# Strided attention on one core: four heads as one contiguous block, keys and values prepared once, one DMA queue in a fixed order

## The chip, the cores and the metric

The kernel runs on one core of a Trainium2 chip. The core has a matmul engine (TensorE, PE in the profile, its weight loads PEld), a vector engine (VectorE, DVE), an engine for activations and copies (ScalarE, ACT), GpSimd (POOL), and SyncE (SP), which here only issues transfers; sixteen DMA engines move data between the device memory and the on-chip memory (SBUF). Matmuls write to a second on-chip memory, PSUM, which has eight banks. The metric is the time of one execution in microseconds (us); lower is better. Before the change it is 152.51 us, the median of three runs (152.01 to 153.02).

## The reference

Each of the 1024 queries of each of the 8 × 12 heads attends to 16 keys, those at every 64th position. All arrays are float32.

```python
batch, heads, seq, dim = (8, 12, 1024, 64)      # stride 64
scale = 1.0 / np.sqrt(dim)
for i in range(seq):
    attend_positions = np.arange(0, seq, stride)
    q = Q[:, :, i:i + 1, :].copy()
    k = K[:, :, attend_positions, :].copy()
    v = V[:, :, attend_positions, :].copy()
    scores = np.einsum('bhqd,bhkd->bhqk', q, k) * scale
    weights = np.exp(scores - np.max(scores, axis=-1, keepdims=True))
    weights = weights / (np.sum(weights, axis=-1, keepdims=True) + 1e-10)
    result[:, :, i, :] = np.einsum('bhqk,bhkd->bhqd', weights, v)[:, :, 0, :]
```

Q and the result are 25.17 MB each; the rows of K and V that are used are 0.39 MB each. Arithmetic is small, so nearly all the data that moves is Q in and the result out.

## The kernel before

The work is cut into 24 groups of four heads (loops over `b` and `g0`). For each group one DMA loads 1 MiB of Q (`qn`, line 111): partition p of 128 holds, for each of the four heads, query rows 8p to 8p+7, so a partition receives four rows of 2 KiB, one from each head. Two small DMAs (lines 116 and 121) load the group's 64 key rows and 64 value rows of 256 bytes. All loads are issued by SP, the store of the result by ACT (line 221).

The values are used as bf16 by reading the upper half of each float32 in place. Per group, in the order in which the program names them:

- Four matmuls (lines 127 and 135) with 0/1 matrices `r_top` and `r_bot` spread the keys (transposed) and the values into a block layout in PSUM, `kv_psum`; ScalarE copies it to SBUF as `kv_sb` (line 144). A pair of query rows sits in one 128-partition column block, so the block layout holds every head's keys twice, for the upper and the lower 64 rows.
- Sixteen 128 × 128 transposes on TensorE (line 154) turn Q into `qt_psum`, which takes two PSUM banks and has one buffer. One ScalarE copy of 2048 columns (line 160) moves it to `qt_all`.
- Four score matmuls (line 166), one for each head, each in its own 32-column strip of the array and 512 columns long. ScalarE takes the exponential with the scale (line 175) into `w1t`. The maximum is not subtracted.
- Four matmuls with a 0/1 selector `s_sel` (line 179) give the sums, and VectorE takes their reciprocals (line 188).
- For each of the four heads, four output matmuls (line 193) with 32 rows of weights and 128 columns, into one PSUM bank of two, and two VectorE multiplies of 256 elements by the reciprocals (line 210), into `out_sb`.

Q has four buffers, `qt_all`, the kv tiles, `w1t` and `out_sb` three each. The order in which each engine runs its instructions is not the order of the program: a planner reorders the work of neighbouring groups, so transposes of one group stand among the output matmuls of another. Waits between engines are set from the tiles that are read and written. A DMA waits at its issuing engine: on SP a load whose buffer is not free holds back what is issued behind it.

Of the kernel before, what the change touches and what calls it, by code (L numbers as in the profile page):

```python
# [11 lines left out]
FP32 = mybir.dt.float32  # L13
BF16 = mybir.dt.bfloat16
# [10 lines left out]

@with_exitstack
def kernel(
# [8 lines left out]
    nc = tc.nc  # L36
# [6 lines left out]
    G = 4  # L43
    RPP = S // P
    NT = RPP // 2
    CH = S // (2 * P)
    assert H % G == 0 and RPP == 8 and NK == 16

    const_pool = ctx.enter_context(tc.tile_pool(name="const", bufs=1))
    qn_pool = ctx.enter_context(tc.tile_pool(name="qn", bufs=4))  # L50
    qt_pool = ctx.enter_context(tc.tile_pool(name="qt", bufs=3))
    kv_pool = ctx.enter_context(tc.tile_pool(name="kv", bufs=3))
    w_pool = ctx.enter_context(tc.tile_pool(name="w", bufs=3))
    out_pool = ctx.enter_context(tc.tile_pool(name="outsb", bufs=3))
    rec_pool = ctx.enter_context(tc.tile_pool(name="rec", bufs=2 * G))
    psum_sc = ctx.enter_context(tc.tile_pool(name="psc", bufs=2, space=bass.MemoryType.PSUM))
    psum_o = ctx.enter_context(tc.tile_pool(name="po", bufs=2, space=bass.MemoryType.PSUM))
    psum_sums = ctx.enter_context(tc.tile_pool(name="psums", bufs=1, space=bass.MemoryType.PSUM))
    psum_qt = ctx.enter_context(tc.tile_pool(name="pqt", bufs=1, space=bass.MemoryType.PSUM))
    psum_kv = ctx.enter_context(tc.tile_pool(name="pkv", bufs=1, space=bass.MemoryType.PSUM))  # L60

    identity = const_pool.tile([P, P], BF16, name="identity")
    make_identity(nc, identity)

    col_idx = const_pool.tile([P, P], I16, name="col_idx")
    nc.gpsimd.iota(col_idx, pattern=[[1, P]], base=0, channel_multiplier=0)
    iota_p = const_pool.tile([P, 1], I16, name="iota_p")
    nc.gpsimd.iota(iota_p, pattern=[[0, 1]], base=0, channel_multiplier=1)  # L68

    p_shr4 = const_pool.tile([P, 1], I16, name="p_shr4")  # L70
    nc.vector.tensor_scalar(  # L71
        out=p_shr4, in0=iota_p, scalar1=4, scalar2=None, op0=ALU.logical_shift_right
    )
    p_shr4_f32 = const_pool.tile([P, 1], FP32, name="p_shr4_f32")
    nc.vector.tensor_copy(out=p_shr4_f32, in_=p_shr4)
    target_i16 = const_pool.tile([P, 1], I16, name="target_i16")
    nc.vector.tensor_scalar(
        out=target_i16, in0=p_shr4, scalar1=16.0, scalar2=None, op0=ALU.mult
    )
    nc.vector.tensor_tensor(out=target_i16, in0=target_i16, in1=iota_p, op=ALU.add)  # L80
    target_f32 = const_pool.tile([P, 1], FP32, name="target_f32")
    nc.vector.tensor_copy(out=target_f32, in_=target_i16)
    target_bot_f32 = const_pool.tile([P, 1], FP32, name="target_bot_f32")
    nc.vector.tensor_scalar(
        out=target_bot_f32, in0=target_f32, scalar1=16.0, scalar2=None, op0=ALU.add
    )

    r_top = const_pool.tile([P, P], BF16, name="r_top")
    nc.vector.tensor_scalar(
        out=r_top, in0=col_idx, scalar1=target_f32, scalar2=None, op0=ALU.is_equal  # L90
    )
    r_bot = const_pool.tile([P, P], BF16, name="r_bot")
    nc.vector.tensor_scalar(
        out=r_bot, in0=col_idx, scalar1=target_bot_f32, scalar2=None, op0=ALU.is_equal
    )

    col_idx8 = const_pool.tile([P, 2 * G], I16, name="col_idx8")
    nc.gpsimd.iota(col_idx8, pattern=[[1, 2 * G]], base=0, channel_multiplier=0)
    s_sel = const_pool.tile([P, 2 * G], BF16, name="s_sel")
    nc.vector.tensor_scalar(  # L100
        out=s_sel, in0=col_idx8, scalar1=p_shr4_f32, scalar2=None, op0=ALU.is_equal
    )

    for b in range(B):
        for g0 in range(0, H, G):
            qn = qn_pool.tile([P, G, RPP, D], FP32, name="qn", tag="qn")
            q_src = _ap_with(
                Q[b, g0],
                [[RPP * D, P], [S * D, G], [1, RPP * D]],
            )  # L110
            nc.sync.dma_start(qn, q_src)
            qn_bf = qn.bitcast(BF16)
            qn_pitch = G * RPP * 2 * D

            k_raw = kv_pool.tile([G * NK, D], FP32, name="k_raw", tag="k_raw")
            nc.sync.dma_start(k_raw, K[b, g0 : g0 + G, ::stride, :])
            k_bf = k_raw.bitcast(BF16)
            k_hi = _ap_with(k_bf, [k_bf.ap[0], [2, D]], extra_offset=1)

            v_raw = kv_pool.tile([G * NK, D], FP32, name="v_raw", tag="v_raw")  # L120
            nc.sync.dma_start(v_raw, V[b, g0 : g0 + G, ::stride, :])
            v_bf = v_raw.bitcast(BF16)
            v_hi = _ap_with(v_bf, [v_bf.ap[0], [2, D]], extra_offset=1)

            kv_psum = psum_kv.tile([P, 2 * P], FP32, name="kv_psum", tag="kv_psum")
            for hp, rmat in enumerate((r_top, r_bot)):
                nc.tensor.matmul(  # L127
                    kv_psum[64 * hp : 64 * hp + D, 0:P],
                    lhsT=k_hi,
                    rhs=rmat[0 : G * NK, :],  # L130
                    start=True,
# [125 lines left out]
```

## Time and profile before

The profiled execution has a span of 150.7 us from the first to the last instruction. No separate time of that execution is given beside its span; the median of the runs is 152.51 us, 1.8 us above it.

| | |
|---|---|
| median of 3 runs | 152.51 us (152.01 to 153.02) |
| profiled execution, span | 150.7 us |
| TensorE matmul busy | 126.9 us (84%), 1056 instructions |
| VectorE busy | 79.9 us (53%) |
| ScalarE busy | 67.0 us (44%) |
| GpSimd busy | 1.1 us (1%) |
| moved by DMA | 51.29 MB, mean 340 GB/s over the span |

How to read it. The page has the busy time of each engine, the span cut into 40 slices (busy tenths of each engine, and GB/s), the DMA queues, the chain of work that ended last, and the costliest groups of instructions. A group's row reads: line, engine, operation, output<-input by name, shapes, count, then total busy us and the mean ns of one, then the idle time of the engine just before these instructions and what ended most of it. The chain is followed back from the last instruction, at each step to what released it; in order of time, each piece has its start, its length, and the engine and line. A window's row has, for a stretch of the span, the busy us of each engine with its count of instructions, the granted TensorE clock, the share of the sixteen DMA engines that was busy, and GB/s. A timeline's row has a start, a length, the engine and line, what is written and read, and how many instructions are merged. Matmuls overlap in the array, so the busy time of TensorE is more than the time that the array needs, and idle time of an engine that is not the bottleneck costs nothing.

### The profile page before, as it was taken

How to read it: one execution, taken by the hardware profiler on the slowest of the kernel's cores; microseconds unless marked ns; L12 is line 12 of the kernel's file. 1: busy time of each engine (PE TensorE's matmuls, PEld its weight loads, DVE VectorE, ACT ScalarE, POOL GpSimd, SP SyncE). 2: the span in 40 equal slices, each digit the busy share in tenths (PEclk: the TensorE clock that was granted, in tenths of full speed). 3: DMA queues.
4: the chain of work that ended last, by engine and by line, in shares of the span. 5: the costliest groups of instructions: out<-in, count | busy, mean ns of one | idle time of the engine just before them, and what ended most of it. 6: DMA issues, size and time to landing. Idle time of an engine off the chain costs nothing.

```text
span 150.7 us, 2715 instructions
## 1 busy us (share of the span) xinstructions
PE 126.9 (84%) x1056; PEld 84.2 (56%) x1056; DVE 79.9 (53%) x225; ACT 67.0 (44%) x73; POOL 1.1 (1%) x9
## 2 busy tenths in 40 slices
PE   0279889989989989989989989989989989987630
PEld 0246656646646647647647647647647647646210
DVE  3004575565565565565565565564564564574650
ACT  3063547147147147147147147147147147147100
POOL 2000000000000000000000000000000000000000
DMA  4999999999999999999999999999999987257266
GB/s 133 347 358 367 363 391 407 280 316 398 397 405 404 408 397 404 406 398 379 397 388 376 385 364 378 384 388 357 387 372 358 389 313 295 102 182 278 99 232 226
DMA packets 29196, 51.29 MB, mean 340 GB/s; under 512 B 4608, under 2 KB 4608, under 8 KB 29184
## 3 DMA queue, kind: packets, MB, share of 16 engines
q1 hardware_dynamic: 16512, 25.96, 49.3%
q10 hardware_dynamic: 12672, 25.17, 43.5%
q8 instruction: 8, 0.13, 0.3%
q14 instruction: 4, 0.03, 0.1%
HBM read 25.95 MB, written 25.17 MB: 339 GB/s over the span
## 4 chain that ended last, share of the span: by engine, by line
PE 73%; ACT 17%; DMA 4%; DVE 2%; issue 1%; DVEq 0%; ACTq 0%
PE qt_psum L154 31%; PE out L193 21%; ACT qt_all L160 16%; PE scores L166 13%; DMA qn<-in_Q_dram 4%; PE kv_psum L127 4%; PE kv_psum L135 3%; DVE out_sb L210 2%; PE sums_psum L179 2%; ACT w1t L175 0%; DVEq L252 0%; ACTq L160 0%; ACTq L175 0%
## 5 line engine op out<-in xcount | busy, mean ns | idle before, releaser
L210 DVE TENSOR_TENSOR out_sb<-out,recip 128x256 f32<-128x256 f32 x192 | 70.0, 418 | 20.6 <-PE out L193 20.2
L160 ACT COPY qt_all<-qt_psum 128x2048 bf16<-128x2048 bf16 x24 | 44.8, 1866 | 34.9 <-PE qt_psum L154 30.8
L154 PE MATMUL qt_psum<-identity,qn 128*128 128x128 bf16 x384 | 49.4, 311 | 6.4 <-DMA qn<-in_Q_dram 6.4
L154 PEld LDWEIGHTS <-qn 128*128 128x128 bf16 x384 | 37.8, 141 | 20.8 <-DMA qn<-in_Q_dram 11.2
L193 PE MATMUL out<-kv_sb,w1t 32*128 32x128 bf16 x384 | 42.7, 302 | 2.0 <-DVE out_sb L210 1.7
L188 DVE RECIPROCAL recip<-sums_psum 128x32 f32<-128x32 f32 x24 | 8.6, 358 | 43.2 <-PE sums_psum L179 43.2
L193 PEld LDWEIGHTS <-w1t 32*128 32x128 bf16 x384 | 24.2, 125 | 12.0 <-DVE out_sb L210 8.9
L175 ACT ACTIVATE w1t<-scores 128x512 bf16<-128x512 f32 x24 | 14.3, 597 | 32.7 <-PE scores L166 17.9
L166 PE MATMUL scores<-qt_all,kv_sb 128*32 128x512 bf16 x96 | 21.5, 604 | 7.8 <-ACT qt_all L160 7.8
L166 PEld LDWEIGHTS <-kv_sb 128*32 128x32 bf16 x96 | 5.0, 101 | 14.2 <-issue 13.9
L144 ACT CAST kv_sb<-kv_psum 128x256 bf16<-128x256 f32 x24 | 8.9, 372 | 6.4 <-PE kv_psum L135 6.4
L127 PEld LDWEIGHTS <-k_raw 64*64 64x64 bf16 x48 | 5.9, 124 | 6.3 <-issue 2.6
L127 PE MATMUL kv_psum<-r_top,k_raw 64*64 64x128 bf16 x24 | 7.5, 312 | 0.8 <-DMA k_raw<-in_K_dram 0.8
L179 PEld LDWEIGHTS <-w1t 128*128 128x128 bf16 x96 | 7.3, 127 | 1.3 <-ACT w1t L175 1.3
L179 PE MATMUL sums_psum<-s_sel,w1t 128*128 128x8 bf16 x96 | 7.0, 179 | 0.8 <-ACT w1t L175 0.8
L127 PE MATMUL kv_psum<-r_bot,k_raw 64*64 64x128 bf16 x24 | 7.4, 310 | 0.0
L135 PE MATMUL kv_psum<-v_raw,r_bot 64*128 64x64 bf16 x24 | 5.6, 233 | 0.0
L135 PE MATMUL kv_psum<-v_raw,r_top 64*128 64x64 bf16 x24 | 5.5, 231 | 0.0
L135 PEld LDWEIGHTS <-r_bot 64*128 64x128 bf16 x24 | 2.5, 103 | 2.8
L135 PEld LDWEIGHTS <-r_top 64*128 64x128 bf16 x24 | 2.5, 102 | 2.8
L144 ACT ACT_TABLE_LOAD x1 | 1.3, 1283 | 0.7 <-PEq L238 0.7
L71 DVE TENSOR_SCALAR p_shr<-iota_p 128x1 int16<-128x1 int16 x1 | 0.2, 156 | 1.6 <-POOL iota_p L68 1.6
(17 smaller groups left out, 2.9 us busy)
## 6 DMA issues: line engine op xcount, KB each, us to landing
qn<-in_Q_dram SPq DMA_DIRECT2D x24, 1024.0 KB, 8.6
out_dram<-out_sb ACTq DMA_DIRECT2D x24, 1024.0 KB, 8.3
k_raw<-in_K_dram SPq DMA_DIRECT2D x24, 16.0 KB, 7.8
v_raw<-in_V_dram SPq DMA_DIRECT2D x24, 16.0 KB, 7.4
```

Of the source, the lines that this page charges most:

```text
L71: nc.vector.tensor_scalar(out=p_shr4, in0=iota_p, scalar1=4, scalar2=None, op0=ALU.logical_shift_right)
L127: nc.tensor.matmul(kv_psum[64 * hp : 64 * hp + D, 0:P], lhsT=k_hi, rhs=rmat[0 : G * NK, :], start=True, stop=True, tile_position=(0, 64 * hp),
L135: nc.tensor.matmul(kv_psum[:, P + 64 * hp : P + 64 * hp + D], lhsT=rmat[0 : G * NK, :], rhs=v_hi, start=True, stop=True, tile_position=(0, 0),
L144: nc.scalar.copy(kv_sb, kv_psum)
L154: nc.tensor.transpose(qt_psum[:, (gi * NT + t) * P : (gi * NT + t + 1) * P], lhsT, identity,)
L160: nc.scalar.copy(qt_all, qt_psum)
L166: nc.tensor.matmul(scores[32 * gi : 32 * gi + 32, :], lhsT=kv_sb[:, 32 * gi : 32 * gi + 32], rhs=qt_all[:, 512 * gi : 512 * (gi + 1)], sta ...
L175: nc.scalar.activation(out=w1t, in_=scores, func=AF.Exp, bias=0.0, scale=scale)
L179: nc.tensor.matmul(sums_psum[:, c, :], lhsT=w1t[:, c * P : (c + 1) * P], rhs=s_sel, start=True, stop=True, tile_position=(0, 0),)
L188: nc.vector.reciprocal(recip, sums_psum)
L193: nc.tensor.matmul(out1[:, c, :, :], lhsT=w1t[32 * gi : 32 * gi + 32, c * P : (c + 1) * P], rhs=kv_sb[32 * gi : 32 * gi + 32, P : 2 * P], ...
L210: nc.vector.tensor_tensor(out=dst, in0=out1[:, :, e, :], in1=recip_b, op=ALU.mult,)
```

## The change

The kernel is written anew around the same arithmetic.

- **Blocks.** Four heads of 1024 queries are 4096 consecutive query rows, 1 MiB in one piece. Partition p now holds 32 consecutive query rows, one run of 8 KiB. The head of a row therefore depends on the partition (32 partitions for a head) and no longer on the place within it.
- **Loads and stores.** Q has eleven buffers and the result nine. All DMAs are issued by SP: keys, values, eleven loads, then for each group its store and the load of the group eleven ahead. The result leaves in an order in which a partition has two runs of 4 KiB.
- **Keys and values once.** The used rows of all 96 heads come in two DMAs of 1536 rows of 256 bytes, ahead of Q. GpSimd makes permutations from the identity, and bf16 copies. Twelve matmuls and six ScalarE copies put the keys into `k_t`; four matmuls and sixteen VectorE multiplies by a 0/1 `mask` put the values into `v_bd`, for each group a 128 × 256 matrix that has each head's values in the rows of that head alone.
- **Weights.** The exponentials are written into one of three buffers, zeroed once, by two activations of 64 partitions each, so that the two halves stand on the diagonal of each 128 × 128 block and zeros stand elsewhere. Score matmuls read Q in runs of 32 columns. Sums take eight matmuls of 4 columns instead of four of 8; outputs eight of 128 rows and 256 columns instead of sixteen of 32 rows and 128 columns; VectorE's multiplies are four of 512 elements instead of eight of 256.
- **Order.** `tc.manual_schedule()` leaves the order as written. For group g: sums, outputs 0 and 1, scores of g+1, output 2, the first half of the transposes of g+2, output 3, the second half. The transposed Q goes through PSUM in halves of 1024 columns with two buffers; output banks are three.

```diff
...
+    HG = 4
+    NG = B * H // HG
+    NC = NG // 2
+    SD = S * D
+    assert B * H == NG * HG and S == 1024 and D == 64 and NK == 16
+    QBUFS = 11
+    OBUFS = 9
+    const = ctx.enter_context(tc.tile_pool(name="const", bufs=1))
+    qn_pool = ctx.enter_context(tc.tile_pool(name="qn", bufs=QBUFS))
+    out_pool = ctx.enter_context(tc.tile_pool(name="outsb", bufs=OBUFS))
+    qt_pool = ctx.enter_context(tc.tile_pool(name="qt", bufs=2))
+    rec_pool = ctx.enter_context(tc.tile_pool(name="rec", bufs=2))
+    psum_qt = ctx.enter_context(tc.tile_pool(name="pqt", bufs=2, space=bass.MemoryType.PSUM))
     psum_sc = ctx.enter_context(tc.tile_pool(name="psc", bufs=2, space=bass.MemoryType.PSUM))
...
+    psum_o = ctx.enter_context(tc.tile_pool(name="po", bufs=3, space=bass.MemoryType.PSUM))
+    psum_s = ctx.enter_context(tc.tile_pool(name="psm", bufs=1, space=bass.MemoryType.PSUM))
+    ctx.enter_context(tc.manual_schedule())
+    k_raw = const.tile([P, NC, D], FP32, name="k_raw")
+    v_raw = const.tile([P, NC, D], FP32, name="v_raw")
+    kv_src = [[stride * D, P], [2 * HG * SD, NC], [1, D]]
+    nc.sync.dma_start(k_raw, _ap_with(K, kv_src))
+    nc.sync.dma_start(v_raw, _ap_with(V, kv_src))
+    qn = {}
+    def load(g):
+        qn[g] = qn_pool.tile([P, 32 * D], FP32, name="qn", tag="qn")
+        nc.sync.dma_start(qn[g], _ap_with(Q, [[32 * D, P], [1, 32 * D]], g * HG * SD))
+    for g in range(QBUFS):
+        load(g)
+    identity = const.tile([P, P], BF16, name="identity")
     make_identity(nc, identity)
...
+    id_v = identity.rearrange("p (c b a k) -> p c b a k", c=2, b=2, a=2)
+    perm_k = const.tile([P, 2, 2, 2, NK], BF16, name="perm_k")
+    perm_v = const.tile([P, 2, 2, 2, 2, NK], BF16, name="perm_v")
+    for c in range(2):
+        for a in range(2):
+            nc.gpsimd.tensor_copy(out=perm_k[:, c, a], in_=id_v[:, c, :, a])
+    k_dup = const.tile([P, NC, 2, D], BF16, name="k_dup")
+    for e in range(2):
+        nc.gpsimd.tensor_copy(out=k_dup[:, :, e], in_=k_raw)
+    for c in range(2):
+        for a in range(2):
+            for e in range(2):
+                nc.gpsimd.tensor_copy(
+                    out=perm_v[:, c, a, :, e], in_=id_v[:, c, :, a]
+                )
+    v_bf = const.tile([P, NC, D], BF16, name="v_bf")
+    nc.gpsimd.tensor_copy(out=v_bf, in_=v_raw)
+    k_t = const.tile([P, NC, 2, 4, 2, NK], BF16, name="k_t")
+    nc.vector.memset(k_t, 0.0)
+    w_bufs = []
+    for i in range(3):
+        w = const.tile([P, 8, P], BF16, name=f"w{i}")
+        nc.vector.memset(w, 0.0)
+        w_bufs.append(w)
+    iota_p = const.tile([P, 1], I16, name="iota_p")
     nc.gpsimd.iota(iota_p, pattern=[[0, 1]], base=0, channel_multiplier=1)
...
+    slot_i = const.tile([P, 1], I16, name="slot_i")
     nc.vector.tensor_scalar(
...
+        out=slot_i, in0=iota_p, scalar1=4, scalar2=3,
+        op0=ALU.logical_shift_right, op1=ALU.bitwise_and,
+    )
+    slot_f = const.tile([P, 1], FP32, name="slot_f")
+    nc.vector.tensor_copy(out=slot_f, in_=slot_i)
+    col4 = const.tile([P, 4], I16, name="col4")
+    nc.gpsimd.iota(col4, pattern=[[1, 4]], base=0, channel_multiplier=0)
+    s_sel = const.tile([P, 4], BF16, name="s_sel")
     nc.vector.tensor_scalar(
...
+        out=s_sel, in0=col4, scalar1=slot_f, scalar2=None, op0=ALU.is_equal
+    )
+    mask = const.tile([P, 4], FP32, name="mask")
     nc.vector.tensor_scalar(
...
+        out=mask, in0=col4, scalar1=slot_f, scalar2=None, op0=ALU.is_equal
+    )
+    pk = perm_k.rearrange("p c a b k -> p (c a b k)")
+    for n in range(NC // 4):
+        kp = psum_o.tile([P, 4, 2, 4, NK], FP32, name="kp", tag="o")
+        for i in range(4):
+            nc.tensor.matmul(
+                kp[:, i], lhsT=k_dup[:, 4 * n + i].rearrange("p e d -> p (e d)"),
+                rhs=pk, start=True, stop=True,
+            )
+        for e in range(2):
+            h = slice(64 * e, 64 * e + 64)
+            nc.scalar.copy(
+                k_t[h, 4 * n : 4 * n + 4, :, :, e].rearrange("p n c s k -> p (n c s) k"),
+                kp[h].rearrange("p n c s k -> p (n c s) k"),
+            )
+    v_bd = const.tile([P, NC, 2, 4, D], BF16, name="v_bd")
+    for n in range(2):
+        for c in range(2):
+            vp = psum_sc.tile([P, NC // 2, D], FP32, name="vp", tag="sc")
+            nc.tensor.matmul(
+                vp, lhsT=perm_v[:, c].rearrange("p a b e k -> p (a b e k)"),
+                rhs=v_bf[:, 6 * n : 6 * n + 6], start=True, stop=True,
+            )
+            for s in range(4):
+                nc.vector.tensor_scalar(
+                    out=v_bd[:, 6 * n : 6 * n + 6, c, s], in0=vp,
+                    scalar1=mask[:, s : s + 1], scalar2=None, op0=ALU.mult,
                 )
...
+    qt, wt, rec, out_sb = {}, {}, {}, {}
+    def transposes(g, x):
+        if x == 0:
+            qt[g] = qt_pool.tile([P, 2, 8, P], BF16, name="qt", tag="qt")
+        ps = psum_qt.tile([P, 8, P], BF16, name="qt_ps", tag="qt_ps")
+        qb = qn[g].bitcast(BF16)
+        for i in range(8):
+            nc.tensor.transpose(
+                ps[:, i],
+                _ap_with(qb, [qb.ap[0], [2, P]], extra_offset=(8 * x + i) * 2 * P + 1),
+                identity,
+            )
+        nc.scalar.copy(qt[g][:, x], ps)
+    def scores(g):
+        sc = psum_sc.tile([P, 512], FP32, name="sc", tag="sc")
+        q = qt[g]
+        kt = k_t[:, g // 2, g % 2].rearrange("p s e k -> p (s e k)")
+        for j in range(4):
+            a, b = divmod(j, 2)
+            nc.tensor.matmul(
+                sc[32 * j : 32 * j + 32],
+                lhsT=kt[:, 32 * j : 32 * j + 32],
+                rhs=_ap_with(
+                    q, [q.ap[0], [P, 8], [8 * P, 2], [1, 32]],
+                    extra_offset=32 * (2 * b + a),
+                ),
+                start=True, stop=True, tile_position=(0, 32 * j),
+            )
+        w = wt[g] = w_bufs[g % 3]
+        for a in range(2):
+            wa = w[64 * a : 64 * a + 64]
+            nc.scalar.activation(
+                out=_ap_with(wa, [wa.ap[0], [P, 8], [1, 2], [2, 32]], extra_offset=64 * a),
+                in_=sc[64 * a : 64 * a + 64].rearrange("p (t x q) -> p t x q", t=8, x=2),
+                func=AF.Exp, bias=0.0, scale=scale,
+            )
+    def sums(g):
+        sm = psum_s.tile([P, 2, 8, 2], FP32, name="sm", tag="sm")
+        for i in range(8):
+            nc.tensor.matmul(
+                sm[:, :, i], lhsT=wt[g][:, i], rhs=s_sel, start=True, stop=True
+            )
+        rec[g] = rec_pool.tile([P, 2, 16], FP32, name="rec", tag="rec")
+        nc.vector.reciprocal(rec[g], sm.rearrange("p b i e -> p b (i e)"))
+    def outputs(g, c):
+        if c == 0:
+            out_sb[g] = out_pool.tile([P, 2, 16, D], FP32, name="out_sb", tag="out_sb")
+        ps = psum_o.tile([P, 2, 2, 2 * D], FP32, name="o_ps", tag="o")
+        for i in range(2):
+            nc.tensor.matmul(
+                ps[:, :, i], lhsT=wt[g][:, 2 * c + i],
+                rhs=v_bd[:, g // 2, g % 2].rearrange("p s d -> p (s d)"),
+                start=True, stop=True,
+            )
+        nc.vector.tensor_tensor(
+            out=out_sb[g][:, :, 4 * c : 4 * c + 4],
+            in0=ps.rearrange("p b i (e d) -> p b (i e) d", e=2),
+            in1=rec[g][:, :, 4 * c : 4 * c + 4].unsqueeze(3).to_broadcast([P, 2, 4, D]),
+            op=ALU.mult,
+        )
+    def store(g):
+        nc.sync.dma_start(
+            _ap_with(out, [[16 * D, P], [2 * SD, 2], [1, 16 * D]], g * HG * SD),
+            out_sb[g].rearrange("p b i x -> p b (i x)"),
+        )
+    for g in range(2):
+        for x in range(2):
+            transposes(g, x)
+    scores(0)
+    for g in range(NG):
+        sums(g)
+        outputs(g, 0)
+        outputs(g, 1)
+        if g + 1 < NG:
+            scores(g + 1)
+        outputs(g, 2)
+        if g + 2 < NG:
+            transposes(g + 2, 0)
+        outputs(g, 3)
+        if g + 2 < NG:
+            transposes(g + 2, 1)
+        store(g)
+        if g + QBUFS < NG:
+            load(g + QBUFS)
```

More of the change, by code (lines that the diff above doesn't have):

```diff
@@ L42 @@
     P = 128
[L43 to L54, printed above, removed]
@@ L55 @@
-    rec_pool = ctx.enter_context(tc.tile_pool(name="rec", bufs=2 * G))
-    psum_sc = ctx.enter_context(tc.tile_pool(name="psc", bufs=2, space=bass.MemoryType.PSUM))
[L57 to L60, printed above, removed]
@@ L84 @@
     nc.vector.tensor_scalar(
-        out=target_bot_f32, in0=target_f32, scalar1=16.0, scalar2=None, op0=ALU.add
+        out=mask, in0=col4, scalar1=slot_f, scalar2=None, op0=ALU.is_equal
     )
[L88 to L95, printed above, removed]
```

126 lines of the change are left out of this document (removed).

## The prediction

> **What bounds the kernel now.** I read the chain of waits first, in its order of time. The first copy of the transposed Q, and one steady stretch, two of the 24 groups long (start us, length us, what):
>
> ```profile
> 9.29 1.88 ACT qt_all L160
> ...
> 64.93 1.88 ACT qt_all L160
> 66.85 0.62 PE scores L166 x4
> 67.46 1.82 PE qt_psum L154 x16
> 69.28 0.09 PE sums_psum L179 x4
> ...
> 69.92 0.24 PE kv_psum L127
> ...
> 70.76 0.60 PE out L193 x4
> ...
> 76.27 1.88 ACT qt_all L160
> ```
>
> TensorE works, then stands while ScalarE makes its one copy of the transposed Q, then works again. The copy starts at 64.93 and the copy two groups on at 76.27: 11.34 us for two groups, 5.67 us for one. 24 × 5.67 is 136.1, with the 9.3 us before the first copy and a tail of some 5 that is the whole span of 150.7.
>
> Second, are the transfers what holds that rhythm? The windows (busy time of PE, PEld, DVE, ACT, POOL; granted clock; DMA share; GB/s):
>
> ```profile
> 5.00:10.00 5.00, 2.81 (x20) 1.99 (x20) 0.00 (x0) 1.08 (x2) 0.00 (x0) 1.00 1.01 333
> 10.00:20.00 10.00, 9.18 (x83) 6.44 (x83) 4.64 (x14) 5.19 (x7) 0.00 (x0) 1.00 1.06 369
> ...
> 40.00:60.00 20.00, 18.65 (x162) 12.53 (x159) 11.62 (x32) 10.15 (x11) 0.00 (x0) 1.00 1.06 403
> ...
> 120.00:135.00 15.00, 13.67 (x116) 8.87 (x113) 8.94 (x26) 7.33 (x7) 0.00 (x0) 1.00 0.64 238
> ```
> ```profile
> 110.29 1.88 ACT qt_all L160
> ...
> 121.63 1.88 ACT qt_all L160
> ...
> 132.97 1.88 ACT qt_all L160
> ```
>
> No: from 120 on the loads are over and the DMA share falls from 1.06 to 0.64, yet the copies still stand 11.34 apart. So TensorE plus the copy sets the pace. But the DMA engines are full until then, so they are a second wall just behind the first: the page counts
>
> ```profile
> DMA packets 29196, 51.29 MB, mean 340 GB/s; under 512 B 4608, under 2 KB 4608, under 8 KB 29184
> ```
>
> and at the 403 GB/s of 40:60, the best long stretch with both directions, that is 127 us of transfer. Any cure for the first wall meets this one, so I cost three things: the rhythm of the new loop, the transfers, and the new start.
>
> **The new loop, per group.** The rows of single operations:
>
> ```profile
> 13.77 1.42 DVE L210 TENSOR_TENSOR out_sb<-out,recip 128x256 f32<-128x256 f32 x4 [0.18 <-PE out L193]
> 60.79 0.31 PE L193 MATMUL out<-kv_sb,w1t 32*128 32x128 bf16 x1
> 61.03 0.61 PE L166 MATMUL scores<-qt_all,kv_sb 128*32 128x512 bf16 x2
> 61.57 1.35 PE L154 MATMUL qt_psum<-identity,qn 128*128 128x128 bf16 x11
> ```
> ```profile
> L210 DVE TENSOR_TENSOR out_sb<-out,recip 128x256 f32<-128x256 f32 x192 | 70.0, 418 | 20.6 <-PE out L193 20.2
> L160 ACT COPY qt_all<-qt_psum 128x2048 bf16<-128x2048 bf16 x24 | 44.8, 1866 | 34.9 <-PE qt_psum L154 30.8
> L154 PE MATMUL qt_psum<-identity,qn 128*128 128x128 bf16 x384 | 49.4, 311 | 6.4 <-DMA qn<-in_Q_dram 6.4
> ...
> L188 DVE RECIPROCAL recip<-sums_psum 128x32 f32<-128x32 f32 x24 | 8.6, 358 | 43.2 <-PE sums_psum L179 43.2
> ...
> L175 ACT ACTIVATE w1t<-scores 128x512 bf16<-128x512 f32 x24 | 14.3, 597 | 32.7 <-PE scores L166 17.9
> L166 PE MATMUL scores<-qt_all,kv_sb 128*32 128x512 bf16 x96 | 21.5, 604 | 7.8 <-ACT qt_all L160 7.8
> ...
> L144 ACT CAST kv_sb<-kv_psum 128x256 bf16<-128x256 f32 x24 | 8.9, 372 | 6.4 <-PE kv_psum L135 6.4
> ```
>
> *TensorE.* Sixteen transposes stay: 1.82 (chain). Four score matmuls stay: 0.62; their moving operand now comes in runs of 32 elements, which no row shows; between 0 and a doubled stream (+0.4) I take 0, because the weight loads of L154 already read with a stride at full pace. The sums go from 4 to 8: 2 × 0.09 = 0.18. The output matmuls go from sixteen of 32 rows × 128 columns to eight of 128 rows × 256 columns. Eleven transposes take 1.35 us, of which the last shows its 0.311 of latency: (1.35 − 0.31)/10 = 0.104 us per 128 columns, so 0.21 per 256, and 8 × 0.21 = 1.7. The four key/value matmuls (0.24 of them shown above; about 0.8 in all) leave the loop, and so do the switches between 32-row and 128-row tiles: 60.79 to 61.03 is 0.24 for a matmul of 0.104, so such a switch costs some 0.13; two a group are left, around the scores, and the chain's pieces hold them. Sum 1.82 + 0.62 + 0.18 + 1.7 = 4.3.
>
> *ScalarE.* One copy of 2048 columns becomes two of 1024. From 372 ns (256) to 1866 (2048) is 0.834 ns a column, so 1866 − 1024 × 0.834 = 1.01 us each. The exponential becomes two of 64 partitions × 512, at 0.60 each. Together 3.2; the kv cast (0.37) and the issue of stores leave ScalarE.
>
> *VectorE.* Eight multiplies of 256 become four of 512. Four in a row take 1.42, so the pace is (1.42 − 0.42)/3 = 0.33 per 256; twice that is the most, 0.67. 4 × 0.67 + 0.36 = 3.0.
>
> So TensorE leads, if the order lets it run. It writes the scores of the next group after outputs 0 and 1, so the exponential lies beside outputs 2 and 3 and the transposes. The copy of the second half of transposes is the tight one: last transpose starts, 0.31 latency, 1.01 copy, two signals of about 0.06: 1.45 us to the scores that need it, where TensorE has sums, two outputs and the switch in between, 0.18 + 0.86 + 0.13 = 1.17, after the 0.1 of that transpose itself. A stall of 0.1 to 0.2 stays where the whole 1.88 stood. I take 4.45 us a group, against 5.67.
>
> **The transfers.** Bytes are the same: 25.17 MB in, 25.17 out, 0.79 of keys and values, 51.1 MB. Rows become 8 KiB on loads and 4 KiB on stores. No row shows a load or store in rows above 2 KiB, so I take no gain, 403 GB/s: 51.1/0.403 = 127 us. Bounds are the 369 and 333 GB/s of loads on one queue (138 and 153 us), and, below, the best slices of the page:
>
> ```profile
> GB/s 133 347 358 367 363 391 407 280 316 398 397 405 404 408 397 404 406 398 379 397 388 376 385 364 378 384 388 357 387 372 358 389 313 295 102 182 278 99 232 226
> ```
>
> 408, so 125 us. I take 403 and not 369 because the stretch at 369 also carries the 256-byte rows of keys and values, in step with Q.
>
> The Trainium skill (DMA: Bandwidth & Descriptors, "Where 436 GB/s comes from") says that for HBM to SBUF the HBM side binds at about 358 GB/s per core. By that figure the transfers alone would take an estimated 143 us. The trace differs: 403 over 20 us with this one core running; the measurement decides, and the sum stays at 127.
>
> Stores move from ACT's queue to SP's, where store g waits for the last multiply of group g and the load of group g+11 is queued behind it. That costs nothing while eleven Q buffers cover it. Eleven loads and the keys and values are 12.3 MB, 30.6 us of work; group 0 stores at about 27 (below), before they are through, at about 34. From there each finished group adds 2.1 MB, 5.2 us of transfer per 4.45 us of computing, so the queue only grows, until the last load goes out behind store 12. Out buffers (nine) come free in time: store 14, which group 23 waits for, lands near 106, and group 23 writes at 121. A single DMA, with its bytes at 403 taken out, has 3.1 us of latency:
>
> ```profile
> 0.74 5.66 DMA qn<-in_Q_dram
> ```
>
> 5.66 − 1.05/0.403 = 3.06. So the transfers end at 0.7 + 3.1 + 127 = 131, and the span 0.5 later if they bind to the end: 131.3.
>
> **The new start.** Keys and values now come whole, in 3072 rows of 256 bytes ahead of Q. K lands at best after 0.74 + 3.06 + 0.39/0.403 = 4.8; at worst the DMA is as slow as its present median of 7.8 from issue to landing, so 8.5:
>
> ```profile
> k_raw<-in_K_dram SPq DMA_DIRECT2D x24, 16.0 KB, 7.8
> ```
> ```profile
> masks.py:199 POOL TENSOR_SCALAR_AFFINE_SELECT identity<-identity 128x128 bf16<-128x128 bf16 x1 | 0.3, 293 | 0.0
> ...
> L66 POOL IOTA col_idx<- 128x128 int16 x1 | 0.2, 234 | 0.0
> ...
> L75 DVE CAST p_shr_f<-p_shr 128x1 f32<-128x1 int16 x1 | 0.2, 154 | 0.0
> ...
> L98 POOL IOTA col_idx<- 128x8 int16 x1 | 0.1, 136 | 0.0
> ```
>
> I take 6.0. Then GpSimd: two copies of 768 elements, eight of 32, one of 768, and the iota for the mask, which stands behind them all. From 8 to 128 columns an iota grows by 98 ns, 0.82 a column: 0.76 us for 768. The select takes 293 for 128, and 2.3 ns a column from nothing gives 1.8. I take 1.2: 3 × 1.2 + 8 × 0.16 + 0.3 = 5.2, at 11.2. VectorE makes the mask in four small operations of 0.15, 11.8, and then sixteen multiplies of 384 elements, between 0.33 and 0.67, 0.5 each. TensorE is in written order: the last of the four V matmuls needs the first eight multiplies (two score buffers), 15.8, and the first transposes stand behind it, 16.2. Four half groups at ScalarE's 1.01 follow the first 0.9: 21.3; exponential 1.2: group 0's sums start at 22.6. Bounds, from the ends above: 19 to 28. The remaining V multiplies end at 19.8, beside this, and ACT's key copies (six of about 0.6) by 13.
>
> **The sum.** Group 22 and 23 have no transposes to do: after 22 × 4.45 = 97.9 they take 2.6 and 3.8 (exponential, sums, outputs and the last multiplies in a chain). Then the last store, as now:
>
> ```profile
> 142.62 2.87 DVE L210 TENSOR_TENSOR out_sb<-out,recip 128x256 f32<-128x256 f32 x8 [0.18 <-PE out L193]
> ```
>
> 145.49 to 150.7, 5.2 us. So 22.6 + 97.9 + 6.4 + 5.2 = 132.1, against the 131.3 of the transfers: two walls almost in one place. I take 132.2 for the span. The median shown, 152.5, is 1.8 above the profiled span of 150.7, the only profiled time given; so 134.0 us.
>
> **Rivals.**
>
> *TensorE at twice the pace.* The window rows print a granted clock of 1.00 throughout, while a matmul of 512 columns takes 604 ns and one of 128 takes 311: 0.76 ns a column. If denser work halved that, TensorE would need about 2.3 a group, ScalarE's 3.2 would lead, computing would end before 110, and the transfers alone would be left: 131.3 + 1.8 = 133 at 403 GB/s, 131 at 408, less if long rows are cheaper. Against it: the same pace in every stretch at 9.3 busy of 10. Chance 0.1. The Trainium skill (TensorE: Matmul & The Clock Gate, "Single matmul latency") gives (219 + N)/1.2 ns for the cold array, 609 for 512 columns, which the 604 agrees with; by that rule the array has been cold all along.
>
> *One queue is slower than two.* Loads and stores now alternate in one queue, and the trace has one queue alone only at 333 to 369 GB/s. At 369 the transfers take 138.5: 0.7 + 3.1 + 138.5 + 0.5 + 1.8 = 144.6. At 333 it is 153.5 and 159.6, slower than before. It decides for slower, over 154.0, from (154.0 − 6.1) = 147.9 us of transfer, 346 GB/s, down. For it: the only rows of one queue alone. Against: they carry short rows, and the DMA share there is already 1.01 to 1.06. The Trainium skill (DMA: Bandwidth & Descriptors, "Issuing engines are not separate DMA queues") says that a second issuing engine saves only issue time; no run here shows it. Chances: 0.12 for about 145, 0.08 for over 154.
>
> *The fixed order stalls.* If each group loses 0.5 more (strided scores, an exponential that writes every second element, signals), 22 × 0.5 = 11: 145. Or the start is at its bound, +5: 139. Chance 0.12.
>
> **How the numbers follow.** Forecast (both walls near 132, each free by some us): 0.58, 129 to 139. Gate open 0.10, 128 to 134; one queue 0.12 near 145 and 0.08 over 154; stalls 0.12, 139 to 146. 128 to 146 leaves out the slow queue and a little on either side. About 1% is the least that a measurement of this kernel tells from no change: faster by more than that (under 151.0) 0.90, within 0.03 (a queue between 346 and 355 GB/s), slower 0.07.
>
> **What would show it.** In the profile after: ScalarE's copies in pairs, 4.45 apart by group; transfers at a share of 1 to 1.05 and about 400 GB/s from 3 to 127 us with no dip; the first sums near 22.6; a chain of mostly PE at the front and DMA at the end. Wrong, if the GB/s row lies under 370 (one queue), if VectorE's or ScalarE's rows show longer operations than 0.67, 1.01 and 0.60, or if the first sums come after 28.

## The result, and the profile after

The changed kernel takes 130.91 us (median of four runs, 130.87 to 130.92) against 152.31 for the kernel before, measured beside it: a ratio of 0.859, 95% interval 0.857 to 0.861. The forecast was 134.0, in a range of 128 to 146. The profiled execution has a span of 129.1 us. In four of the runs below (two queues, the kernel before with 128 rows, and both with four Q buffers) some executions, the profiled ones among them, took over 1.5% longer than the fastest of the same kernel; medians and ranges are of all executions, ratios of the faster ones alone.

From the page after: the granted clock in tenths, the DMA share and GB/s in 40 slices of 3.2 us, the queues, and the groups that answer to those shown of before.

```profile
PEclk9999997799999999999999999999999999555555
DMA  2999999999999999999999999999999999999980
GB/s 64 273 426 416 419 431 419 421 411 421 415 423 433 405 428 426 414 425 420 419 428 420 416 435 419 419 431 415 420 434 404 420 417 417 419 420 421 420 360 34
...
q1 hardware_dynamic: 13088, 51.12, 97.6%
q8 instruction: 7, 0.11, 0.3%
...
L223 DVE TENSOR_TENSOR out_sb<-o_ps,rec 128x512 f32<-128x512 f32 x96 | 63.2, 689 | 15.2 <-PE o_ps L218 12.8
L178 ACT COPY qt<-qt_ps 128x1024 bf16<-128x1024 bf16 x48 | 46.2, 1015 | 5.2 <-PE qt_ps L173 4.7
L198 ACT ACTIVATE w<-sc 64x512 bf16<-64x512 f32 x48 | 35.3, 736 | 13.1 <-PE sc L186 12.8
L218 PE MATMUL o_ps<-v_bd,w 128*128 128x256 bf16 x192 | 34.2, 284 | 0.0
L173 PE MATMUL qt_ps<-identity,qn 128*128 128x128 bf16 x384 | 31.1, 228 | 0.2 <-ACT qt L178 0.2
...
L186 PE MATMUL sc<-qt,k_t 128*32 128x512 bf16 x96 | 9.8, 396 | 24.3 <-ACT qt L178 24.3
```

The transfers are full and even, about 421 GB/s from the third slice on, and a 512-column matmul takes 396 ns where it took 604. The windows of the kernel after (columns as before):

```profile
20.00:25.00 5.00, 4.22 (x45) 3.05 (x46) 2.98 (x5) 3.13 (x5) 0.00 (x0) 0.66 1.01 419
...
60.00:80.00 20.00, 13.56 (x184) 10.04 (x182) 15.33 (x26) 17.33 (x21) 0.00 (x0) 1.00 1.02 423
...
115.00:120.00 5.00, 0.00 (x0) 0.00 (x0) 0.00 (x0) 0.00 (x0) 0.00 (x0) 0.50 1.03 424
120.00:125.00 5.00, 0.00 (x0) 0.00 (x0) 0.00 (x0) 0.00 (x0) 0.00 (x0) 0.50 1.01 414
```

From 115 on no engine computes, and the DMA engines are still full. Its timeline shows one round of the loop and the last multiplies:

```profile
69.83 1.49 ACT L198 ACTIVATE w<-sc 64x512 bf16<-64x512 f32 x2 [0.50 <-PE sc L186]
71.34 1.93 ACT L178 COPY qt<-qt_ps 128x1024 bf16<-128x1024 bf16 x2
73.76 1.49 ACT L198 ACTIVATE w<-sc 64x512 bf16<-64x512 f32 x2 [0.50 <-PE sc L186]
...
111.57 2.48 DVE L223 TENSOR_TENSOR out_sb<-o_ps,rec 128x512 f32<-128x512 f32 x4
```

A group takes 73.76 − 69.83 = 3.93 us, all of it ScalarE's: 1.49 for the exponentials, 1.93 for the copies, 0.50 of waiting. Computing ends at 111.57 + 2.48 = 114.05, 15 us before the end of the span. So one wall is left, the transfers, and the experiments ask what raised it, what keeps it full, and how far below it the computing lies.

### The profile page after: what moved, and what is told of

It is laid out like the page before. It is cut to its first block, busy times and chain, and to the rows that moved or that the text cites. A ratio compares the mean times of both kernels' runs of the same rounds, so it can differ in the third digit from the quotient of the medians.

```text
span 129.1 us, 2215 instructions
## 1 busy us (share of the span) xinstructions
PE 70.4 (55%) x880; PEld 51.8 (40%) x880; DVE 83.7 (65%) x144; ACT 86.2 (67%) x103; POOL 5.1 (4%) x23
## 4 chain that ended last, share of the span: by engine, by line
ACT 61%; PE 11%; DVE 5%; DMA 3%; issue 3%; POOL 3%; ACTq 1%; DVEq 0%; POOLq 0%
ACT qt L178 34%; ACT w L198 27%; PE sc L186 8%; DVE v_bd L160 3%; DMA k_raw<-in_K_dram 3%; PE qt_ps L173 1%; DVE out_sb L223 1%; POOL k_dup L96 1%; PE o_ps L218 1%; POOL perm_v L100 1%; POOL v_bf L104 1%; ACTq L285 1%; PE sm L207 1%; DVEq L285 0%; PE vp L155 0%
## 5 line engine op out<-in xcount | busy, mean ns | idle before, releaser
L223 DVE TENSOR_TENSOR out_sb<-o_ps,rec 128x512 f32<-128x512 f32 x96 | 63.2, 689 | 15.2 <-PE o_ps L218 12.8
L178 ACT COPY qt<-qt_ps 128x1024 bf16<-128x1024 bf16 x48 | 46.2, 1015 | 5.2 <-PE qt_ps L173 4.7
L198 ACT ACTIVATE w<-sc 64x512 bf16<-64x512 f32 x48 | 35.3, 736 | 13.1 <-PE sc L186 12.8
L218 PE MATMUL o_ps<-v_bd,w 128*128 128x256 bf16 x192 | 34.2, 284 | 0.0
L173 PE MATMUL qt_ps<-identity,qn 128*128 128x128 bf16 x384 | 31.1, 228 | 0.2 <-ACT qt L178 0.2
L173 PEld LDWEIGHTS <-qn 128*128 128x128 bf16 x384 | 27.3, 103 | 3.9 <-issue 2.6
L186 PE MATMUL sc<-qt,k_t 128*32 128x512 bf16 x96 | 9.8, 396 | 24.3 <-ACT qt L178 24.3
L218 PEld LDWEIGHTS <-w 128*128 128x128 bf16 x192 | 14.6, 100 | 6.6 <-issue 5.6
L211 DVE RECIPROCAL rec<-sm 128x32 f32<-128x32 f32 x24 | 8.6, 358 | 9.0 <-PE sm L207 8.9
L207 PE MATMUL sm<-s_sel,w 128*128 128x4 bf16 x192 | 8.5, 166 | 6.7 <-ACT w L198 5.6
L207 PEld LDWEIGHTS <-w 128*128 128x128 bf16 x192 | 6.4, 96 | 10.8 <-ACT w L198 10.8
```

The source lines that it names most:

```text
L173: nc.tensor.transpose(ps[:, i], _ap_with(qb, [qb.ap[0], [2, P]], extra_offset=(8 * x + i) * 2 * P + 1), identity,)
L178: nc.scalar.copy(qt[g][:, x], ps)
L186: nc.tensor.matmul(sc[32 * j : 32 * j + 32], lhsT=kt[:, 32 * j : 32 * j + 32], rhs=_ap_with(q, [q.ap[0], [P, 8], [8 * P, 2], [1, 32]], ext ...
L198: nc.scalar.activation(out=_ap_with(wa, [wa.ap[0], [P, 8], [1, 2], [2, 32]], extra_offset=64 * a), in_=sc[64 * a : 64 * a + 64].rearrange( ...
L207: nc.tensor.matmul(sm[:, :, i], lhsT=wt[g][:, i], rhs=s_sel, start=True, stop=True)
L211: nc.vector.reciprocal(rec[g], sm.rearrange("p b i e -> p b (i e)"))
```

## The experiments

**Transfers alone.** All computing is left out.

```diff
...
     for g in range(NG):
-        sums(g)
...
+        out_sb[g] = out_pool.tile([P, 2, 16, D], FP32, name="out_sb", tag="out_sb")
+        nc.vector.memset(out_sb[g], 0.0)
         store(g)
         if g + QBUFS < NG:
             load(g + QBUFS)
```

> Left out: all computing; the stored tiles are zeroed once each by VectorE. The two small loads, the 24 loads and the 24 stores stay, in the same order on the same queue. Theory (the transfers alone set the end of the changed kernel): within 0.6 us of its 130.9, between 130.3 and 131.5, at 415 to 425 GB/s. Rival (computing decides when the last stores can go): under 128.

Measured: 128.62 us (128.59 to 129.83), 2.3 below the changed kernel, between the theory's time and the rival's. Its page:

```profile
span 126.9 us, 158 instructions
...
GB/s 60 268 426 424 421 416 429 421 421 421 408 433 433 411 431 429 409 435 415 425 434 413 428 430 416 431 429 412 435 417 422 420 422 420 420 424 421 418 424 150
...
q1 hardware_dynamic: 13088, 51.12, 98.9%
```

The transfers alone make 98% of the time. Most of the 2.3 us shows in the last slices: here the rate stands at 424 up to the last slice, while with computing it sinks to 360 and 34. The DMA engines finish apart there: their busy share is 0.59 from 125 to 126 and 0.16 from 126 to 127, while without computing it falls from 0.81 to 0.01 at 125. The page after has a queue that is missing here, `q8 instruction`, seven fetches of instructions that run on the same engines; that they are what makes some engines late is a guess from this, not shown.

**Two queues.** The stores move back to ACT.

```diff
     def store(g):
-        nc.sync.dma_start(
+        nc.scalar.dma_start(
```

> Only the stores move, from SP's queue to ACT's. Theory (row length sets the rate, the number of queues does not): 130 to 132, at 415 to 430 GB/s. Rival (the single queue, in which loads and stores take turns of 1 MiB, is what lifted the rate from 403 to 421): the rate falls back to about 405 and the time goes to 135. A third possibility, that two queues hide what is left between rows: up to 435 GB/s, 127 to 128.

Measured: 135.32 us (134.33 to 138.27), ratio to before 0.887 (0.880 to 0.894). That is the rival's time, but not its reason. From the profiled execution, which took 138.27 us, windows first, then waits (who waited for whom: us in total, times, longest), and ScalarE around the longest of them:

```profile
40.00:60.00 20.00, 12.85 (x117) 8.71 (x115) 10.35 (x18) 11.61 (x15) 0.00 (x0) 0.66 1.01 422
60.00:80.00 20.00, 6.78 (x97) 5.25 (x96) 7.54 (x13) 8.38 (x11) 0.00 (x0) 0.84 1.02 424
...
115.00:120.00 5.00, 3.57 (x54) 2.71 (x51) 4.07 (x7) 4.43 (x7) 0.00 (x0) 1.00 0.66 264
```
```profile
ACT w L198 <- DMA out_dram<-out_sb: 14.1, 2, 11.0
```
```profile
65.40 1.93 ACT L178 COPY qt<-qt_ps 128x1024 bf16<-128x1024 bf16 x2
77.92 0.38 ACTq L231 DMA_DIRECT2D out_dram<-out_sb  x1
78.35 0.72 ACT L198 ACTIVATE w<-sc 64x512 bf16<-64x512 f32 x1 [11.02 <-DMA out_dram<-out_sb]
```

While the queues hold work, the rate is 422 to 424, as with one: the number of queues does not set it. The Trainium skill (DMA: Bandwidth & Descriptors, "Issuing engines are not separate DMA queues") says that DMAs of different issuing engines run on the same 16 DMA engines and that a second issuer saves only the time of issuing; this run agrees. What is lost is ScalarE's time: a store at its head waits until an earlier store has landed, and the exponentials behind it wait along, once for 11.0 us. (In this trace the 50 DMAs share eight completion semaphores; the stores issued at 43.94 and 77.92, after the two waits, go out just when an earlier store with the same semaphore has landed, at 43.9 and 77.8.) Computing ends late, at 131.1, and from 105 on the queues are no longer full (264 GB/s from 115 to 120). The same waits stand on SP in the changed kernel (a store there waits for an earlier one 11 times, 2.1 us at most), where nothing is behind them but other DMAs. The waits are read from one execution, 3 us above the median, so what each is worth in the 135.3 us is not shown.

**Rows of 2 KiB.**

```diff
-        qn[g] = qn_pool.tile([P, 32 * D], FP32, name="qn", tag="qn")
-        nc.sync.dma_start(qn[g], _ap_with(Q, [[32 * D, P], [1, 32 * D]], g * HG * SD))
+        qn[g] = qn_pool.tile([P, 4, 8 * D + 8], FP32, name="qn", tag="qn")
+        nc.sync.dma_start(
+            qn[g][:, :, 0 : 8 * D],
+            _ap_with(Q, [[32 * D, P], [8 * D, 4], [1, 8 * D]], g * HG * SD),
+        )
...
+        for h in range(2):
...
+                    out, [[16 * D, P], [2 * SD, 2], [1, 8 * D]],
+                    g * HG * SD + 8 * D * h,
...
+                out_sb[g][:, :, 8 * h : 8 * h + 8].rearrange("p b i x -> p b (i x)"),
```

> Rows of 2 KiB again on both sides: each Q tile gets four gaps of 32 bytes, so that its 8 KiB row is cut in four, and each store is cut into two DMAs of half a row, 2 KiB in a run. All else stays. Theory (long rows are worth 403 to 421 GB/s): the rate falls to 400 to 408, 51.1 MB take 125 to 128 us instead of 121.5, and the time is 134.5 to 137.5. Rival (one queue in a fixed order is what raised the rate, and rows do nothing): 130.5 to 131.5.

Measured: 136.43 us (136.26 to 136.96), 5.5 above the changed kernel, as the theory had it. Its window:

```profile
60.00:80.00 20.00, 13.24 (x180) 9.93 (x180) 15.33 (x26) 17.33 (x22) 0.00 (x0) 1.00 1.05 407
```

407 GB/s against 423 in the same stretch, in the same order on the same queue: shorter rows cost 3.9% of the rate. The edit also makes two DMAs of each store; with the DMA engines full all the time (a share of 1.05) this should matter little, but no run separates the two. The Trainium skill (DMA: Bandwidth & Descriptors, "Why small descriptors are slow (HBM only)") gives some three cycles of overhead for each packet beside its 32-byte beats; for 2 KiB against 8 and 4 KiB that is an estimated 2.9%, the right direction and near in size.

**More work on ScalarE**, one extra copy per group, of 256 and of 1024 columns.

```diff
         nc.scalar.copy(qt[g][:, x], ps)
+        if x == 1:
+            nc.scalar.copy(spare, ps[:, 0:2])
...
+            nc.scalar.copy(spare, ps[:, 0:8])
```

> Added: one more ScalarE copy of 256 columns per group, 0.37 us by the copy rows, inside ScalarE's loop of 3.94 us. Theory (transfers set the end; computing ends 14 us before it): computing ends 22 x 0.37 = 8 us later, near 122, the time stays within 0.5 us of 130.9. Rival (ScalarE's loop sets the end): 138 to 139.

> Added to the changed kernel: one more ScalarE copy of 1024 columns per group, 1.0 us. With the extra 256 columns, 0.28 us of 0.37 went into ScalarE's 0.50 us of waiting; so the loop becomes 3.42 + 0.97 + 0.22 = 4.6 us, close to the 4.45 of the prediction. Theory (the later of two walls counts): computing ends at 114.05 + 22 x 0.67 = 128.8, the last store then needs some 4.5 us, and the time is 134 to 137. Rival (transfers hide it all): 131.

Measured: 131.09 (130.69 to 131.38) and 131.09 (131.01 to 131.22). The first is as expected in time, but for less reason: the copy went into the 0.50 us of waiting, of which 0.22 is left, the loop stays at 3.93, and computing ends at 114.8 instead of the expected 122. Of the second, both the loop and the time were missed. Its timeline:

```profile
71.50 1.50 ACT L201 ACTIVATE w<-sc 64x512 bf16<-64x512 f32 x2
73.02 1.93 ACT L179 COPY qt<-qt_ps 128x1024 bf16<-128x1024 bf16 x2
74.83 1.03 ACT L181 COPY spare<-qt_ps 128x1024 bf16<-128x1024 bf16 x1
75.73 0.75 ACT L201 ACTIVATE w<-sc 64x512 bf16<-64x512 f32 x1
...
120.76 2.48 DVE L226 TENSOR_TENSOR out_sb<-o_ps,rec 128x512 f32<-128x512 f32 x4
```

The loop is 4.23 us, not 4.6, since all of the waiting is taken up, and computing ends at 123.2: nine us later than in the changed kernel, for 0.2 us of time. A loop of 4.2 us costs next to nothing here.

**What lets TensorE run fast.** First in the kernel before, with 128-row output matmuls; its outputs are sums over four heads.

```diff
-                        lhsT=w1t[32 * gi : 32 * gi + 32, c * P : (c + 1) * P],
-                        rhs=kv_sb[32 * gi : 32 * gi + 32, P : 2 * P],
+                        lhsT=w1t[:, c * P : (c + 1) * P],
+                        rhs=kv_sb[:, P : 2 * P],
...
-                        tile_position=(32 * gi, 0),
+                        tile_position=(0, 0),
```

> The kernel before, with one edit: each output matmul takes all 128 rows of weights and values instead of the 32 of its head, so that the outputs are sums over four heads. Columns, counts and order stay. Question: what lets TensorE run at twice the pace in the changed kernel (a 512-column matmul of 396 ns instead of 604). Theory (full 128-row matmuls do it, not how tightly TensorE is packed, since the kernel before had 93% of its windows busy and stayed slow): the 512-column row falls to about 396 ns, the loop of 5.67 us shortens to 4.2 to 4.9, and the time falls to 132 to 140, near the transfers' 51.1 MB at 403 GB/s. Rival (denser or steadier work does it): the rows stay at 604 and 311 ns, and the time falls only by the tile switches that go, to 147 to 152.

Then in the changed kernel the other way, with 32 rows and with 64 (the same edit with 0:64), so that most of each output, or half of it, is left out.

```diff
-                ps[:, :, i], lhsT=wt[g][:, 2 * c + i],
-                rhs=v_bd[:, g // 2, g % 2].rearrange("p s d -> p (s d)"),
-                start=True, stop=True,
+                ps[:, :, i], lhsT=wt[g][0:32, 2 * c + i],
+                rhs=v_bd[0:32, g // 2, g % 2].rearrange("p s d -> p (s d)"),
+                start=True, stop=True, tile_position=(0, 0),
```

> The changed kernel, with one edit: its output matmuls take the first 32 rows of weights and values instead of 128, so that most of each output is left out. Columns, counts and order stay; switches between 32-row and 128-row tiles come in, about six a group of some 0.13 us at the slow pace. Theory (128-row matmuls let TensorE run fast): TensorE stays slow, 604 ns for 512 columns; its loop is 4.33 plus four more switches, 4.9 us; computing ends near 24 + 22 x 4.9 + 4 = 136, and the time is 138 to 144. Rival (density does it): rows near 396 ns and 130.5 to 132.

> The changed kernel with output matmuls of 64 rows instead of 128; half of each output is left out. If the number of rows in use opens TensorE's fast pace, 64 lies between: a 512-column matmul between 396 and 604 ns on average, with a granted clock that changes back and forth, and 131 to 138. If only a full array counts: as with 32 rows, 137 to 138. If 64 is enough: 131.

Measured: 143.07 us (140.81 to 144.46; ratio 0.929, 0.922 to 0.936), 137.73 (137.56 to 138.53), and 138.58 in a single run. From the page of the kernel before with 128 rows (an execution of 144.46 us), of the changed kernel with 32, and of the changed kernel with the extra copy of 1024 columns from above:

```profile
PEclk9999999999965995559999998579968689599955
...
L166 PE MATMUL scores<-qt_all,kv_sb 128*32 128x512 bf16 x96 | 16.1, 450 | 5.8 <-ACT qt_all L160 5.3
```
```profile
PEclk9999997555555555555555555555555555555555
...
L186 PE MATMUL sc<-qt,k_t 128*32 128x512 bf16 x96 | 14.6, 593 | 0.0
```
```profile
PEclk9999999999999599995589975799855999599655
```

The pace follows the edit both ways: with 128 rows the kernel before is at full clock much of the time, and with 32 (or 64, 595 ns) the changed kernel stays at half, although TensorE is busier (85% of the span against 55). So a packed TensorE does not open the fast pace by itself. The edit also removes or adds the switches between tile sizes, and no run separates the two. Nor do the rows alone decide: with the extra copy, TensorE does the same 128-row work in a loop of 4.23 us instead of 3.93, and falls back to half the clock again and again (0.50 from 60 to 64), where it held the full clock from 25 to 109 without the copy. How densely the work comes counts too, then, which is what the prediction's first rival supposed. Three sizes missed their expectation: the kernel before reaches 143 only, with DMA waits at half of its chain (52%); the loop with 32 rows is 4.72 us, not 4.9, and the time with it 137.7, just under the 138 to 144; and 64 rows took 138.6, not 137 to 138.

**Buffers**: four Q buffers and three for the result, as before the change, then each alone.

```diff
-    QBUFS = 11
-    OBUFS = 9
+    QBUFS = 4
+    OBUFS = 3
```

> The changed kernel with four Q buffers and three result buffers instead of eleven and nine, as many as the kernel before has. Theory (the deep buffers keep the DMA engines full while keys and values are prepared): keys, values and four loads are moved by 16, and the fifth load waits behind the first store, issued at 25: 9 to 11 us of idle transfers, and more later because loads wait behind stores. 140 to 146. Rival (buffers are deeper than needed): 131.

> The changed kernel with four Q buffers and still nine result buffers. Theory (the Q buffers are what is missing with four and three: the load of group g+4 stands behind store g and is needed two groups later, so a landing of some 7 us and the work after it repeat every two groups): 150 to 160, as with four and three. Rival (the result buffers are what is missing): 138 to 144, only the 9 to 11 us of idle transfers at the start.

> The changed kernel with eleven Q buffers and three result buffers. The first stores stand behind eleven loads and land near 36, so that group 3 waits some 4 us for a result buffer, and later groups go in step with the transfers, which stay full. Theory (Q buffers matter, result buffers hardly): 131 to 138. Rival (result buffers matter as much): 145 to 160.

Measured: 160.21 us (154.2 to 163.49) with both; 158.97 (156.07 to 163.72; ratio to before 1.029, 1.022 to 1.037) with four Q buffers; 136.91 (136.75 to 137.00) with three for the result. With four Q buffers the new kernel is slower than the old one, and the run with both is far over its expected 140 to 146. The slices and the costliest wait of the run with four and nine, in an execution of 163.72 us:

```profile
GB/s 108 334 425 364 0 4 204 269 423 401 375 405 358 362 356 424 293 365 404 250 344 421 306 377 388 237 333 422 307 360 424 248 350 418 272 359 190 256 274 252
...
L173 PE MATMUL qt_ps<-identity,qn 128*128 128x128 bf16 x384 | 42.8, 280 | 40.4 <-DMA qn<-in_Q_dram 40.1
```

and what SP does in it:

```profile
25.23 0.40 SPq L231 DMA_DIRECT2D out_dram<-out_sb  x1
25.74 0.40 SPq L78 DMA_DIRECT2D qn<-in_Q_dram  x1
28.34 0.39 SPq L231 DMA_DIRECT2D out_dram<-out_sb  x1
28.83 0.49 SPq L78 DMA_DIRECT2D qn<-in_Q_dram  x1
35.99 0.40 SPq L231 DMA_DIRECT2D out_dram<-out_sb  x1
36.48 0.42 SPq L78 DMA_DIRECT2D qn<-in_Q_dram  x1
```

Two slices stand empty while keys and values are prepared, and afterwards the rate does not stay full: each load is issued behind a store that waits for computing (SP's stores wait 87.5 us in all for the multiplies), which waits for an earlier load (40.1 us of TensorE's waits). With three result buffers the rate stays near 420 to the 31st slice:

```profile
GB/s 78 281 422 425 422 427 427 410 417 411 428 419 422 426 422 411 436 421 409 427 420 419 432 414 420 431 420 419 426 415 420 353 370 318 275 245 238 257 330 221
...
L223 DVE TENSOR_TENSOR out_sb<-o_ps,rec 128x512 f32<-128x512 f32 x96 | 60.8, 685 | 38.5 <-DMA out_dram<-out_sb 31.3
```

Six microseconds are lost there, with multiplies that wait for a result buffer (31.3 us of VectorE's waits name the store) and a rate that falls from the 32nd slice on.

**Exponentials without the pattern**; they land at other places, so the output is not the attention.

```diff
-                out=_ap_with(wa, [wa.ap[0], [P, 8], [1, 2], [2, 32]], extra_offset=64 * a),
-                in_=sc[64 * a : 64 * a + 64].rearrange("p (t x q) -> p t x q", t=8, x=2),
+                out=wa[:, 4 * a : 4 * a + 4].rearrange("p t m -> p (t m)"),
+                in_=sc[64 * a : 64 * a + 64],
```

> The changed kernel with the exponentials read and written as plain runs of 512, so that they land at other places and the output is not the attention. Disputed: why an exponential of 64 partitions by 512 takes 736 ns where one of 128 by 512 took 597 before. Theory (the pattern, above all every second element of 2 bytes on writing, costs it): 597 ns, ScalarE's loop shorter by 0.28 us, time 131. Rival (the form, or 64 partitions): 736 again.

Measured, in a single run: 131.19 us, and

```profile
L198 ACT ACTIVATE w<-sc 64x512 bf16<-64x512 f32 x48 | 28.4, 591 | 13.6 <-PE sc L186 13.0
```

591 ns: the pattern costs 0.145 us an instruction. The time does not move, which is a third sign that ScalarE's loop does not set it.

## Why the prediction was right, and where it was off

The time came out right because the transfers, one of the forecast's two walls, set it and were priced within about 2 us. In part this was luck: the other wall was not where the forecast put it, and two wrong terms in the price of the transfers partly cancel.

*What bounds the kernel before* held: a loop of TensorE and one long copy, with the transfers as a second wall close behind. Taking the first away gave the second.

*The new loop* was wrong in its leader. The step that took TensorE at 4.3 us and a loop of 4.45 rested on the pace of the rows before. The pace doubled at about 25 us, ScalarE led, and the loop is 3.93. Two of the prediction's own signs failed with it: the pairs of copies do not stand 4.45 apart, and ScalarE's and VectorE's rows show operations longer than it allowed. That is the first rival, to which the forecast gave one chance in ten; its sum, 131 to 133 us, lies nearer the result than the forecast's own. The Trainium skill (TensorE: Matmul & The Clock Gate, "Single matmul latency") gives, by its formulas for a full-array matmul, an estimated 379 ns for 512 columns on a warm array (the fast pace) and 609 on a cold one (the slow pace); the 396 after and 604 before come near the two. The printed clock of 1.00 in the windows of before was no evidence: the row of durations was, and I weighed "busy yet slow" as a reason against, where the experiments show that a busy TensorE can stay slow: 85% busy with 32 rows, 593 ns. ScalarE's term was off too: 0.60 for an exponential measured 0.74, of which the last experiment shows the pattern as the cause; the copies (1.01 forecast, 1.015 measured) and VectorE's multiplies (at most 0.67, measured 0.689 alone, 0.64 in a row) came out near.

This error did not decide the time. With a loop of 4.23 the kernel takes 131.09 and with 4.72 (32 rows) 137.73, so with 4.45, between them, the transfers and the computing would by this estimate have stood close together, as forecast. As it is, computing ends at 114.05, and with a tail of 5 us it would be done at 119, 10 us before the transfers. Where computing does end late, the forecast's tail holds: with 32 rows the last multiplies end at 131.1 and the span at 136.1, 5.0 us later (5.2 forecast).

*The transfers* were mis-sized by two terms that pull against each other. "I take no gain" for long rows: the rate taken was 403 GB/s and it measured 421, some 5.4 us on 51.1 MB, and the experiment with 2 KiB rows gives back 5.5. Left out of the sum was the end, where the DMA engines finish apart, 2.3 us against transfers alone, and that keys and values in 256-byte rows are slower than the mean (the second slice stands at 273). The forecast put the span of this wall at 131.3; it is 129.1. A chain of mostly PE and then DMA, the last of its signs, did not come: the page's chain after is ACT 61%, PE 11%, DMA 3%, and its shares add up to 87%: the 15 us after the last multiply are not in them. That the transfers set the end is seen in the windows and in the experiments, not in that chain.

*The new start* came out 1.8 us early: sums at 20.8 against 22.6, inside the bounds, since K landed at 4.9 instead of 6.0 and GpSimd's copies took 0.83 instead of 1.2.

*One queue costs nothing while eleven buffers cover it* was right, and more hangs on it than the step says: with four Q buffers instead of eleven the kernel takes 28 us more, and with the stores on ACT 4.4 more. Four Q buffers on two queues were not tried in the changed kernel. The rival of a slow single queue is refuted: 418 to 424 GB/s on one.

*The sum* of 134.0 was 3.1 too high, because both walls were put too far out, the transfers by 2 and the computing by 13; the later of the two, the transfers, decided.

## What to carry to other kernels

When two walls stand close together, price both, and then look for what the later one needs to stay full: here not the faster loop but buffers deep enough that loads never wait behind a store that waits for computing. Issue stores from an engine that has nothing else to do, since a DMA that must wait at its issuer holds up everything behind it there. And read a matmul's pace from its duration, not from the printed clock, before taking it over into a new loop.

## What the runs showed of the hardware that was not expected

The fast pace of TensorE did not come from being busy alone. At 85% busy with 32-row or 64-row output matmuls it stayed at 593 to 595 ns for 512 columns, and at 55% busy with 128-row ones it ran at 396. With 128-row ones it held from 25 to 109 us in a loop of 3.93 us, and broke off repeatedly in one of 4.23. Transposes took part in the fast pace once it was there (311 ns before, 228 after).

One queue sustains 421 GB/s with loads and stores taking turns, and falls to 407 with 2 KiB rows; two queues reach the same 422 to 424.

An exponential that writes every second 2-byte element takes 736 ns where a plain one takes 591.
